# Attention scores over all 128 rows of TensorE, softmax sums applied behind the value products, and keys projected feature by feature, in a four-stage transformer kernel

## The chip, the cores and the metric

The kernel runs on one core of a Trainium2 chip. The metric is the device time of one execution in microseconds (us). Before the change three runs took 2884.61, 2885.17 and 2885.28 us; the median is 2885.17.

## What is computed

512 tokens of 1024 features pass through two layers of a block with three branches (a convolution, neighbourhood attention, window attention) that also sees 256 context tokens, then through a recurrent layer (LRU), a feed-forward layer, a layer of native sparse attention (NSA) and a second feed-forward layer. Everything is fp32. What the change touches is the attention. In short:

```python
# window attention: 8 query heads of 64, 2 key heads; blocks of 128 queries see 384 keys and the context
s_w = einsum('bqkgd,bskd->bkgqs', q_n, k_n) * scale          # masked to |distance| <= 128
s_c = einsum('bqkgd,bnkd->bkgqn', q_n, k_ctx) * scale
p = sink_softmax(concatenate([s_w, s_c], -1), sink)          # e / (sum(e) + exp(sink - m))
o = p[..., :span] @ v_n + p[..., span:] @ v_ctx

# neighbourhood attention: 8 heads, a learned bias, softmax over the neighbourhood and the context
# context tokens (first layer only): plain attention among themselves

# NSA: 16 query heads, 4 key heads; three softmaxes per query, mixed by gates
s = einsum('bgrqd,bgqkd->bgrqk', q, k) - slope[head] * distance     # causal
o = g0 * o_compressed + g1 * o_selected + g2 * o_window
```

At 512 tokens all eight blocks are selected and the window holds all tokens, so both of the last NSA softmaxes are causal attention over all earlier tokens.

## The kernel before

**Precision.** Weights, projections and scores are split: a value x becomes hi (x rounded to the type fp32r) and lo (x - hi, rounded again). A product is three matmuls, hi*hi + hi*lo + lo*hi; these are lines 141 to 143 (features on the partitions, up to 512 tokens as columns) and 152 to 154 (tokens on the partitions, 256 features as columns). `load_w` (line 117) loads a weight tile into `wr` through SP's queue, ScalarE rounds it to `wh` and VectorE subtracts to `wl`; the tags `wh` and `wl` have four buffers each. Transposes and the products of probabilities with values are plain fp32.

**Scores.** A head has 64 features. Two heads lie on the two halves of the partitions. `scores` (line 512, window attention and the context's own) and the NSA's `scores` (line 1490) issue for each of the three partial products one matmul of 64 rows per head, alternating the halves. In window attention a unit is one block of 128 queries: blocks 0 and 3 with both heads (256 context columns and 256 band columns), blocks 1 and 2 with one head at a time (256 and 384 columns). A group is one pair of heads with all its blocks, eight groups in all; the first layer has four more of two context blocks, with 256 columns each. Neighbourhood attention has its own matmuls of 512 columns at line 544, and line 517 for its context blocks.

**Softmax.** `att_sm` (line 562) takes the maximum on VectorE, adds the bias and takes the maximum again in one instruction, exponentiates on ScalarE with the sum as a by-product, inverts the sum and multiplies the probabilities by it (line 598). `att_tr` transposes them, `pv` multiplies with the values into `o`, and `finish` (line 668) multiplies `o` into the gate `U` in place.

**NSA.** `kv` projects the keys token by token (`nt_group`, 256 columns), scales them on ScalarE into both halves of `kraw`, transposes them (line 1397) and splits them into `KS`. `queries` makes the queries of a pair of heads, split into `Q`, and scales the table of distances by the two slopes into `M`. For each pair the loop at the end of `nsa` runs eight units (two branches b, query blocks 1, 3, 2, 0) and a compressed one: `scores`, `softmax`, and AHEAD units later `close` (transposes at line 1571, and for the compressed unit the products with the values at 1555 and 1559). Units have max(128*(qb+1), 256) columns: 256, 512, 384, 256. The projection of the next pair's queries is woven in as filler.

**What sets the order.** The program interleaves generators: `weave` runs a main generator and advances a filler in proportion to the cost that each step of the main one reports (ratios RA, RB and, in NSA, 0.32). The framework then schedules the instructions of all engines by dependences and its own cost estimates, so the order on an engine is not that of the source. Each engine's queue runs in order.

## Time and profile before

| | |
|---|---|
| median of three runs | 2885.17 us |
| the profiled execution, its own time | 2888.56 us |
| its span, first to last instruction | 2886.7 us |
| matmuls on PE busy | 2849.4 us, 99% |
| weight loads on PE busy | 2328.9 us, 81% |
| VectorE (DVE) busy | 1931.7 us, 67% |
| ScalarE (ACT) busy | 1119.9 us, 39% |
| GpSimd (POOL) busy | 4.4 us |
| mean granted clock of TensorE | 0.994 of full |

Matmuls are pipelined: a row's duration holds the time through the array, and the next one starts before it ends. What a matmul costs a full queue is the distance from its start to the start of the next. Attention of the block lies at about 110 to 480 us (first layer) and 1060 to 1262 us (second layer), the NSA's at 2227 to 2440 us; most of the rest is projections.

### The profile page before, as it was taken

The numbers are of one execution on the slowest core, as the hardware profiler recorded it, in microseconds if no ns is written. First come the engines' busy times: TensorE is split into PE (matmuls) and PEld (weight loads), VectorE is DVE, ScalarE is ACT, GpSimd is POOL, SyncE is SP. The second block draws the span as 40 slices with busy tenths as digits, with TensorE's granted clock in tenths as the row PEclk, the third lists the DMA queues.
The fourth block names the chain that finished last, engine by engine and source line by source line (L and its number), as shares of the span: only waits on it lengthen the run. The fifth ranks groups of instructions, "written<-read, shape, count | busy, mean of one in ns | idle before, by whom it ended". The sixth has DMA issues, their size and how long they took to land.

```text
span 2886.7 us, 41652 instructions
## 1 busy us (share of the span) xinstructions
PE 2849.4 (99%) x15936; PEld 2328.9 (81%) x15936; DVE 1931.7 (67%) x4663; ACT 1119.9 (39%) x2226; POOL 4.4 (0%) x9
## 2 busy tenths in 40 slices
PE   9999999999999999999999999999999999999998
PEld 7887877888887988778888878888888666888886
DVE  5768788994545667999747866546543777663663
ACT  4434453122222444542334742223333776322222
POOL 0000000000000000000000000000000000000000
PEclk9999999999999999999999999999999999999999
DMA  6111011321344222113233232232242001233322
GB/s 233 59 60 51 30 38 59 103 66 66 124 133 159 70 78 64 35 60 99 95 113 106 86 105 95 88 109 95 86 140 93 23 16 53 93 97 93 102 90 79
DMA packets 80119, 248.70 MB, mean 86 GB/s; under 512 B 9008, under 2 KB 16560, under 8 KB 79920
## 3 DMA queue, kind: packets, MB, share of 16 engines
q1 hardware_dynamic: 75312, 236.07, 25.2%
q10 hardware_dynamic: 4608, 9.96, 1.1%
q8 instruction: 126, 2.06, 0.3%
q14 instruction: 73, 0.60, 0.1%
HBM read 239.71 MB, written 4.19 MB: 84 GB/s over the span
## 4 chain that ended last, share of the span: by engine, by line
PE 89%; DVE 5%; issue 3%; ACT 2%; DMA 1%; POOL 0%; POOLq 0%; SPq 0%; ACTq 0%; DVEq 0%
PE g L141 21%; PE g L143 21%; PE g L142 21%; PE g L152 3%; PE g L154 3%; PE g L153 3%; PE s L517 2%; PE g L1555 1%; PE o L637 1%; PE t L613 1%; PE t L610 1%; PE s L1506 1%; PE s L544 1%; PE t L1571 1%; PE s L277 1%
## 5 line engine op out<-in xcount | busy, mean ns | idle before, releaser
L127 ACT CAST wh<-wr 128x1024 fp32r<-128x1024 f32 (+2 forms) x392 | 392.2, 1002 | 827.9 <-PE g L142 583.7
L141 PE MATMUL g<-Hh,wh 128*128 128x512 f32 x1736 | 689.7, 397 | 0.5 <-DVE Yb L1302 0.4
L142 PE MATMUL g<-Hl,wh 128*128 128x512 f32 x1736 | 681.0, 392 | 0.0
L143 PE MATMUL g<-Hh,wl 128*128 128x512 f32 x1736 | 680.3, 392 | 0.0
L128 DVE TENSOR_TENSOR wl<-wr,wh 128x1024 fp32r<-128x1024 f32 (+2 forms) x392 | 454.7, 1160 | 290.0 <-ACT wh L127 289.3
L141 PEld LDWEIGHTS g<-Hh,wh 128*128 128x128 f32 x1736 | 326.2, 188 | 73.7 <-issue 6.0
L143 PEld LDWEIGHTS g<-Hh,wl 128*128 128x128 f32 x1736 | 325.8, 188 | 71.8 <-issue 2.3
L142 PEld LDWEIGHTS g<-Hl,wh 128*128 128x128 f32 x1736 | 326.5, 188 | 64.1 <-issue 1.0
L152 PE MATMUL g<-wh,Hh 128*128 128x256 f32 x640 | 187.0, 292 | 1.3 <-ACT vn L774 1.3
L943 DVE SCALAR_TENSOR_TENSOR cv<-apad,cv 128x499 f32<-128x499 f32 (+25 forms) x305 | 187.2, 664 | 0.5
L154 PE MATMUL g<-wh,Hl 128*128 128x256 f32 x640 | 182.5, 286 | 0.0
L153 PE MATMUL g<-wl,Hh 128*128 128x256 f32 x640 | 182.3, 285 | 0.0
L141 PE MATMUL g<-fh,wh 128*128 128x512 f32 x384 | 149.4, 389 | 0.0
L142 PE MATMUL g<-fl,wh 128*128 128x512 f32 x384 | 149.4, 389 | 0.0
L143 PE MATMUL g<-fh,wl 128*128 128x512 f32 x384 | 149.4, 389 | 0.0
L152 PEld LDWEIGHTS g<-wh,Hh 128*128 128x128 f32 x640 | 122.6, 192 | 9.3 <-issue 5.5
L154 PEld LDWEIGHTS g<-wh,Hl 128*128 128x128 f32 x640 | 122.0, 191 | 4.2 <-issue 2.5
L153 PEld LDWEIGHTS g<-wl,Hh 128*128 128x128 f32 x640 | 122.6, 192 | 1.3 <-issue 0.8
L1323 DVE TENSOR_TENSOR fxp<-g,nb 128x512 f32<-128x512 f32 x48 | 33.2, 692 | 127.5 <-PE g L143 127.5
L581 ACT ACTIVATE pr<-s,m 128x512 f32<-128x512 f32 (+1 forms) x128 | 80.8, 634 | 77.0 <-DVE m L579 66.4
L1215 DVE TENSOR_TENSOR Xs<-Xs,g 128x512 f32<-128x512 f32 x48 | 33.0, 688 | 113.3 <-PE g L143 113.2
L141 PE MATMUL g<-Ch,wh 128*128 128x256 f32 x352 | 101.0, 287 | 0.0
(414 smaller groups left out, 5275.2 us busy)
## 6 DMA issues: line engine op xcount, KB each, us to landing
wr<-in_ffn_w_in_dram SPq DMA_DIRECT2D x96, 512.0 KB, 3.6
wr<-in_w_in_t_dram SPq DMA_DIRECT2D x88, 512.0 KB, 3.6
wr<-in_ffn_w_out_dram SPq DMA_DIRECT2D x64, 384.0 KB, 3.1
wada<-in_w_ada_dram SPq DMA_DIRECT2D x45, 512.0 KB, 6.0
wr<-in_w_in_n_dram SPq DMA_DIRECT2D x32, 512.0 KB, 3.7
wr<-in_lru_w_in_dram SPq DMA_DIRECT2D x20, 512.0 KB, 3.6
wr<-in_w_o_dram SPq DMA_DIRECT2D x16, 512.0 KB, 3.8
bt<-in_nab_dram SPq DMA_DIRECT2D x48, 128.0 KB, 2.5
```

The lines of the kernel that those rows point to most:

```text
L127: nc.scalar.copy(h[:, :n], r[:, :n])
L128: nc.vector.tensor_sub(lo[:, :n], r[:, :n], h[:, :n].bitcast(F32))
L141: mm(o, a, hi(k), start=k == 0, stop=False)
L142: mm(o, a, lo(k), start=False, stop=False)
L143: mm(o, b, hi(k), start=False, stop=k == KT - 1)
L152: mm(o, h, w[k][0], start=k == 0, stop=False)
L153: mm(o, h, w[k][1], start=False, stop=False)
L154: mm(o, lo(k)[:, t0:t0 + P], w[k][0], start=False, stop=k == KT - 1)
L517: nc.tensor.matmul(dst[i], Q[sl, a, qi, q0:q0 + P], K_[sl, b, ki, k0:k0 + kn], start=a + b == 0, stop=a == 1)
L581: AC.activation(pr, un["S"][i][:, :nb + 256], AF.Exp, bias=m[:, 2:3], accum_out=m[:, 3:4])
L943: V.scalar_tensor_tensor(d, src, wc, d, op0=ALU.mult, op1=ALU.add)
L1323: V.tensor_mul(xp[:, 2:514], o, rb)
```

## The change

- **Window attention and NSA scores use all 128 rows.** The queries are stored per head, with hi on one half of the partitions and lo on the other, and the keys are on both halves. One matmul then sums (hi + lo) * key; one with the keys' hi and one with their lo make the score, two matmuls per head instead of three. For this the halves that belong on the other partitions are moved by DMA: `swap` on GpSimd's queue for window attention, two transfers on SP's queue per pair of heads for NSA. Where a window unit has 256 band columns, one matmul of 512 columns takes band and context. Neighbourhood attention keeps its 64-row scores.
- **Probabilities are not normalised** in the block's attention. The sums of a group are kept side by side (`su`); `parts` inverts them once per group and spreads them over the features by matmuls with the identity, 64 columns of the array each, 8 per group (4 for a context group). `finish` multiplies them into the gate, and then the product with the values. The sink's exponential is also taken once per group. In window attention maximum and bias become one instruction over both parts, with zeros as the bias of the context.
- **NSA queries carry 0.125/slope**; the table of distances is used as it is, and the score is scaled by the slope behind the sum. The two scaled copies `M` and `Mc` are gone.
- **NSA keys are projected feature by feature** (128 features, 512 tokens as columns), so they need no transpose; a DMA on GpSimd's queue copies each to the other partitions. Weights are rearranged to match.
- **NSA's normalisation** moves from VectorE to GpSimd; half of the copies of transposed probabilities move from ScalarE to VectorE. Every fourth probability tile comes from tag `wl`. Units with 256 columns share one PSUM tile for both heads.
- AHEAD goes from 2 to 3, the NSA filler's ratio from 0.32 to 0.45, the early convolution taps' rate ET from 0.4 to 0.6. The `ones` tile shrinks to two columns.

```diff
@@ window queries: head i of a pair, hi on its own half, lo to the other
+            def to_T2_nat(raw, dst, g, tmp):
...
+                    for i, hi, lo in ((0, dst[:, 2 * pr, 0:S], tmp[:, pr]), (1, tmp[:, pr], dst[:, 2 * pr + 1, 0:S])):
+                        sl = slice(64 * i, 64 * i + 64)
+                        for (h, b), (l_, _) in zip(nat(hi[sl], tv[sl], g), nat(lo[sl], tv[sl], g)):
+                            AC.copy(h, b)
+                            V.tensor_sub(l_, b, h.bitcast(F32))
+                if g == 1:
+                    swap(dst.rearrange("p (a i) n -> p a i n", i=2), tmp, slice(0, S))
+            def swap(d4, x, c):
+                nc.gpsimd.dma_start(out=d4[64:128, :, 0, c].bitcast(F32), in_=x[0:64].bitcast(F32))
+                nc.gpsimd.dma_start(out=d4[0:64, :, 1, c].bitcast(F32), in_=x[64:128].bitcast(F32))
@@ scores
+                if not na:
+                    for i in heads:
+                        for b in range(2):
+                            kk = K_[:, b, ki, k0[0]:k0[0] + kn]
...
+                            nc.tensor.matmul(dst[i], Q[:, 2 * qi + i, q0:q0 + P], kk, start=b == 0, stop=b == 1)
+                    return
@@ att_sm
+                        for x, bias, to in todo:
+                            V.tensor_tensor_reduce(out=x, in0=x, in1=bias, scale=-1.0, scalar=mx,
+                                                   op0=ALU.add, op1=ALU.min, accum_out=to)
...
-                    rc = k.small("rc", 1)
-                    V.reciprocal(rc, tot)
...
-                        V.tensor_scalar(pr, pr, rc, None, op0=ALU.mult)
@@ new
+            def parts(grp, sinks):
...
+                V.reciprocal(y, su)
+                t = k.t_()[:, :nq * P]
+                for q in range(nq):
+                    for i in range(2):
+                        nc.tensor.matmul(t[64 * i:64 * i + 64, q * P:(q + 1) * P],
+                                         y[:, 2 * q + i:2 * q + i + 1].to_broadcast([P, 64]), k.ident,
+                                         start=True, stop=True)
+                return t
@@ attend, close
-                                finish(o, U[:, 2 * u + gr["pr"]], gr["cq"], natural)
+                                t = parts(gr, co[:, C_SINK + h0:C_SINK + h0 + 2] if natural else None)
+                                finish(t, U[:, 2 * u + gr["pr"]], gr["cq"], natural, 0.5)
+                                finish(o, U[:, 2 * u + gr["pr"]], gr["cq"], natural, 1.0)
@@ nsa, kv
-                    w = win(2 * b)
...
-                                nc.tensor.transpose(t[:, gg * P:(gg + 1) * P], raw[:, gg].rearrange("p u d -> p (u d)"), k.ident)
...
+                        o = yield from gemm_(k.load_w(a["nsa_w_k"][2 * b + f], 8, P), P, hh, hl)
+                        kr = pool.tile([P, S], F32, tag="kraw", name=k.nm("kraw"))
+                        V.tensor_mul(kr, o, rb)
+                        for i in range(2):
+                            sl, to = slice(64 * i, 64 * i + 64), slice(64 - 64 * i, 128 - 64 * i)
+                            d = KS[b][:, :, 2 * f + i]
+                            k.split(d[sl, 0], d[sl, 1], kr[sl])
+                            nc.gpsimd.dma_start(out=d[to].bitcast(F32), in_=d[sl].bitcast(F32))
@@ nsa, queries
-                V.scalar_tensor_tensor(qf, o, 0.125, rb, op0=ALU.mult, op1=ALU.mult)
...
-                    AC.activation(M[:, i], al, AF.Copy, scale=slopes[2 * f + i])
...
+                V.scalar_tensor_tensor(qf, o, co[:, D_SL + f:D_SL + f + 1], rb, op0=ALU.mult, op1=ALU.mult)
...
+                k.split(Q[0:64, 0], qx[0:64], qf[0:64])
+                k.split(qx[64:128], Q[64:128, 1], qf[64:128])
+                nc.sync.dma_start(out=Q[64:128, 0].bitcast(F32), in_=qx[0:64].bitcast(F32))
+                nc.sync.dma_start(out=Q[0:64, 1].bitcast(F32), in_=qx[64:128].bitcast(F32))
@@ nsa, scores
-                for x, y in ((0, 0), (0, 1), (1, 0)):
-                    for i in range(2):
-                        nc.tensor.matmul(S_[i][:, :nn], Q[sls[i], x, qb * P:(qb + 1) * P], KS[b][sls[i], y, g, :nn],
-                                         start=x + y == 0, stop=x == 1)
+                for i in range(2):
+                    for y in range(2):
+                        nc.tensor.matmul(S_[i][:, :nn], Q[:, i, qb * P:(qb + 1) * P], KS[b][:, y, g, :nn],
+                                         start=y == 0, stop=y == 1)
@@ nsa, softmax
-                    V.tensor_scalar(pr[:, :nk], pr[:, :nk], m[:, 2:3], GT[:, qb, h:h + 1], op0=ALU.mult, op1=ALU.mult)
+                    G.tensor_scalar(pr[:, :nk], pr[:, :nk], m[:, 2:3], GT[:, qb, h:h + 1], op0=ALU.mult, op1=ALU.mult)
```

How the instructions stand on PE, before and after, at three places. Names are tile<-moving operand,stationary operand; the numbers at a tile's name count the tiles.

First, window attention of the first layer, before: the filler of the next queries (152 to 154) and the scores of block 1 for the first head.

```order
L153 MATMUL g_3911<-wl_3808,Hh_134 128x256
L154 MATMUL g_3911<-wh_3807,Hl_135 128x256
L517 MATMUL s_3959<-kw_3080,qw_3505 128x256 x3
L517 MATMUL s_3960<-kw_3080,qw_3505 128x384 x3
L152 MATMUL g_3911<-wh_3807,Hh_134 128x256
```

The same place after (line 560 is now the scores' matmul); the second head of block 0 stands ahead of it, with band and context in one.

```order
L154 MATMUL g_3880<-wh_3771,Hl_135 128x256
L560 MATMUL s_3886<-kw_3030,qw_3455 128x512 [waits DMASW1_49]
L560 MATMUL s_3886<-kw_3030,qw_3455 128x512
L560 MATMUL s_3905<-kw_3030,qw_3455 128x256 x2
L560 MATMUL s_3906<-kw_3030,qw_3455 128x384 x2
```

Three matmuls per head and set became two, and the first to read a swapped half waits for a transfer of GpSimd's queue.

Second, the start of NSA's attention, before: the end of the first queries' projection and the first scores.

```order
L142 MATMUL g_20940<-Hl_19611,wh_20936 128x512
L143 MATMUL g_20940<-Hh_19610,wl_20937 128x512
L1506 MATMUL s_20975<-KS_20083,nQ_20967 128x256 [waits Activation_49]
L1506 MATMUL s_20976<-KS_20083,nQ_20967 128x256 [waits PE_49]
L1506 MATMUL s_20975<-KS_20083,nQ_20967 128x256
L1506 MATMUL s_20976<-KS_20083,nQ_20967 128x256
```

After, the same place (line 1604 is now the scores' matmul):

```order
L143 MATMUL g_20104<-Hh_18918,wl_20101 128x512
L141 MATMUL g_20161<-Hh_18918,wh_20157 128x512 [waits Activation_49]
L142 MATMUL g_20161<-Hl_18919,wh_20157 128x512
L143 MATMUL g_20161<-Hh_18918,wl_20158 128x512 [waits DVE_49]
L141 MATMUL g_20161<-Hh_18918,wh_20157 128x512
L142 MATMUL g_20161<-Hl_18919,wh_20157 128x512
L143 MATMUL g_20161<-Hh_18918,wl_20158 128x512
L141 MATMUL g_20161<-Hh_18918,wh_20157 128x512
L1604 MATMUL s_20139<-KS_19391,nQ_20131 128x256 [waits DMAHW6_49,DMASW4_49,PE_49]
L1604 MATMUL s_20139<-KS_19391,nQ_20131 128x256
```

Seven matmuls of the second pair's projection now stand ahead of the first score, which waits for the swap on SP's queue (DMAHW) and the copy of the keys (DMASW).

Third, the end of the second window group, second layer, before: the products with the values, then scores of the next group.

```order
L658 MATMUL o_13232<-PT_13098,misc_11922 64x256 x2
L517 MATMUL s_13270<-kw_11944,qw_12528 128x256 [waits Activation_49]
L517 MATMUL s_13271<-kw_11944,qw_12528 128x256
```

After, the end of the same group: the products, `parts` (line 681), then transposes of the next queries.

```order
L749 MATMUL o_12657<-PT_12562,misc_11493 64x256 x2
L681 MATMUL t_12676<-ident,rc_12670 64x128 [waits PE_49]
L681 MATMUL t_12676<-ident,rc_12670 64x128 x7
L527 MATMUL t_12706<-ident,raw_12542 128x128 [waits PE_49]
L527 MATMUL t_12706<-ident,raw_12542 128x128 x3
```

The eight matmuls of line 681 are new; the next group's scores come later, behind more of the filler.

## Rows read from the trace of the kernel before

**Rows 1.** The page, part 1: busy us, share of the span, instructions.
```profile
PE 2849.4 (99%) x15936; PEld 2328.9 (81%) x15936; DVE 1931.7 (67%) x4663; ACT 1119.9 (39%) x2226; POOL 4.4 (0%) x9
```

**Rows 2.** Waits of PE: who waited for whom, us, times, longest.
```profile
PE t L505 <- DVE raw L841: 3.0, 6, 0.9
PE s L1506 <- ACT nQ L209: 2.8, 2, 1.4
```

**Rows 3.** Line 1506: durations (min/median/max ns), first and last start, forms.
```profile
L1506 PE MATMUL s<-KS,nQ x384: 272/382/793, 2226.8 to 2421.9; 64*128 64x256 f32 x96, 64*128 64x512 f32 x48, 64*128 64x384 f32 x48
```

**Rows 4.** Timeline of PE, NSA attention: start us, us, instruction, count.
```profile
2287.52 0.79 PE L1506 MATMUL s<-KS,nQ 64*128 64x384 f32 x6
2288.25 0.66 PE L1571 MATMUL t<-ident,pr 128*128 128x128 f32 x4
2288.66 0.48 PE L141 MATMUL g<-Hh,wh 128*128 128x512 f32 x1
2288.97 0.40 PE L142 MATMUL g<-Hl,wh 128*128 128x512 f32 x1
...
2289.53 0.62 PE L1506 MATMUL s<-KS,nQ 64*128 64x256 f32 x6
2290.08 1.19 PE L1571 MATMUL t<-ident,pr 128*128 128x128 f32 x8
...
2293.26 0.96 PE L1506 MATMUL s<-KS,nQ 64*128 64x512 f32 x6
2294.15 0.33 PE L1571 MATMUL t<-ident,pr 128*128 128x128 f32 x1
```

**Rows 5.** Timeline of PE, projection of NSA keys and values, 256 columns.
```profile
2206.12 0.28 PE L152 MATMUL g<-wh,Hh 128*128 128x256 f32 x1
2206.24 0.28 PE L153 MATMUL g<-wl,Hh 128*128 128x256 f32 x1
```

**Rows 6.** Timeline of PE, window attention: blocks 1 and 2; then a pair.
```profile
354.25 0.61 PE L517 MATMUL s<-kw,qw 64*128 64x256 f32 x3
354.79 0.50 PE L142 MATMUL g<-Hl,wh 128*128 128x512 f32 x1
...
357.54 0.78 PE L517 MATMUL s<-kw,qw 64*128 64x384 f32 x3
358.25 0.44 PE L613 MATMUL t<-ident,pr 128*128 128x128 f32 x2
...
411.30 0.39 PE L142 MATMUL g<-Hl,wh 128*128 128x512 f32 x1
411.52 0.40 PE L143 MATMUL g<-Hh,wl 128*128 128x512 f32 x1
411.85 0.98 PE L517 MATMUL s<-kw,qw 64*128 64x256 f32 x12
412.76 0.50 PE L141 MATMUL g<-Hh,wh 128*128 128x512 f32 x1
```

**Rows 7.** Timeline of PE, NSA: compressed values, then the filler.
```profile
2284.24 1.09 PE L1559 MATMUL g<-nb,VC 124*64 124x128 f32 x13
2285.26 0.50 PE L141 MATMUL g<-Hh,wh 128*128 128x512 f32 x1
```

**Rows 8.** Timeline of all engines at the first NSA scores.
```profile
2225.36 0.69 DVE L1481 SCALAR_TENSOR_TENSOR qf<-g,nb 128x512 f32<-128x512 f32 x1 [7.45 <-PE g L143]
2226.09 0.62 ACT L209 CAST nQ<-qf 128x512 fp32r<-128x512 f32 x1 [5.35 <-DVE qf L1481]
...
2226.76 1.35 PE L1506 MATMUL s<-KS,nQ 64*128 64x256 f32 x8 [1.43 <-ACT nQ L209]
```

**Rows 9.** The page's DMA issues: tiles, count, KB each, us to landing.
```profile
bt<-in_nab_dram SPq DMA_DIRECT2D x48, 128.0 KB, 2.5
...
cD<-ct SPq DMA_DIRECT2D x4, 256.0 KB, 3.9
```

**Rows 10.** Groups of POOL: line, operation, tiles, forms, count, busy us, mean ns.
```profile
L1616 POOL TENSOR_TENSOR ht<-Xs,nb 128x512 f32<-128x512 f32 x3 | 3.7, 1271 | 2876.7 <-ACT nb L195 2876.7
```

211 lines of the change are left out of this document (134 added, 77 removed).

## The prediction

> **What bounds the kernel now.** I read the page's first part, then the waits of PE, then the timeline of PE in the stages that the diff touches. The page puts matmuls on PE in 99% of the span, DVE in 67%, ACT in 39% [rows 1]. That could be an engine that looks busy while its matmuls stretch, so the waits are the test: on the lines of attention the largest are 3.0 us in six waits and 2.8 us in two [rows 2], out of 2886.7 us. PE is the bound, its queue runs in order, and the change is priced by the distance from one PE start to the next. Work of DVE, ACT or POOL counts only where PE would wait for it.
>
> The timeline gives these distances. In a projection with 512 columns the next matmul starts 0.22 us later (411.30 to 411.52, [rows 6]); I use 0.225. With 256 columns it is 0.12 [rows 5]. For 384 columns no full-array row exists; between these two I estimate 0.172. Scores are matmuls on 64 rows (64*128 in the rows), two heads on the two halves. Six of 256 columns fill 0.55 us before the next instruction starts, six of 384 0.73, six of 512 0.89 [rows 4]. Three of 256 columns, of one head alone, fill 0.54, three of 384 0.71, and twelve of 256 0.91 [rows 6]. So two heads do share the array: six cost what three cost. But every visit to the half array has a price. From the last full matmul to the first score it is 0.33 instead of 0.22 (411.52 to 411.85, [rows 6]), 0.11 more, and the end is late too: three slots of 0.12 are 0.36, yet 0.54 to 0.55 pass.
>
> Here a rule of the Trainium skill speaks against the change. "TensorEngine Tiling (Array Packing)", Theoretical Speedup, gives a contraction of 64 or less up to twice the throughput when the array is split by rows, so going back to the full array, 4 slots for 3, would cost time. The rows agree that pairs overlap, and disagree on the balance for visits this short. The first rival below is what remains if the price of a visit doesn't go away.
>
> **Change part by part.** The times are made against the profiled execution (span 2886.7, own time 2888.56) and the difference is then taken off the median of 2885.17, which lies 3.4 below that execution.
>
> *Window attention scores (wa_att).* Before: 32 head-units alone (blocks 1 and 2 of eight groups, two heads), each with three matmuls of 256 and three of 384; 16 pairs (blocks 0 and 3) with twelve of 256; 8 context pairs with six of 256. A unit alone costs 0.11 + 0.54 + 0.11 + 0.71 = 1.47, after it 2 x 0.12 + 2 x 0.172 = 0.58: 0.89 less. In 8 of the 32 the two sets stand back to back and pay one visit, so there I count 0.68. That is 24 x 0.89 + 8 x 0.68 = 26.8. A pair costs 0.11 + 0.91 = 1.02, after it four of 512, 0.90: 16 x 0.12 = 1.9. A context pair costs 0.11 + 0.55, after it 0.48: 8 x 0.18 = 1.4. **Together -30.** If all units stood back to back it would be -25.
>
> *NSA scores.* 64 units: 32 of 256 columns save 0.66 - 0.48 = 0.18, 16 of 384 save 0.84 - 0.69 = 0.15, 16 of 512 save 1.00 - 0.90 = 0.10. **-9.8.** If the visit cost only its entry, 0.11, and the late end stayed whatever stands there, this part would lose about 2.
>
> *NSA keys.* Before: 192 matmuls of 256 columns, 23.0, and eight sets of four transposes. A set costs 0.41, and the projection matmul behind it takes 0.31 instead of 0.225 (2288.25 to 2288.97, [rows 4]): 0.50. After: 96 matmuls of 512 columns, 21.6, no transposes. **-1.4 - 4.0 = -5.4.** The copies of the keys to the other partitions go out on POOL's queue. The value projection of the same branch, 96 matmuls of 0.12 or 11.5 us, follows on PE before any score asks for them, so I take them at nothing; without that cover each branch would cost a landing, 2.5 to 3.9 [rows 9].
>
> *Sums behind the value products (parts).* It adds 8 matmuls of 128 columns to each of 16 groups and 4 to each of 8 context groups: 160, into half the columns (128*64). No row is this form; the nearest are the 124*64 ones of NSA, 13 in 1.02 = 0.078 [rows 7]. **+12.5.** Ends: half a transpose, 0.05 (two at a time), 8; a whole one, 0.10, 16 (four in 0.41, [rows 4]).
>
> *DVE and ACT.* Gone are a normalisation per head-unit and its small operations; added are one product with PSUM per group and three small operations. PE waits 3.0 us at most for any one DVE line here [rows 2], so I take this at nothing; it can only help.
>
> *NSA queries.* Slopes go into the queries, which removes two scaled copies of the table per pair of heads from ACT: nothing, PE covers it. But each pair's second halves now go through two DMAs on SP's queue. For the first pair nothing covers them. Before: the first score starts 1.40 after the product qf [rows 8]. After: qf 0.69, cast 0.62 [rows 8], a subtraction like qf's, 0.69, then a landing between 2.5 and 3.9 [rows 9], so 4.5 to 5.9. The order shows seven projection matmuls (1.6) put ahead of that score. Net 1.5 to 2.9 later; with the second head's half a cast later I take **+2.4**. For the later pairs the next projection ends several us earlier than the scores, so one of the two waits of 1.4 [rows 2] goes: **-1.4**. Behind a swap on SP stand weight loads that are two tiles ahead: nothing.
>
> *Window queries* are swapped by POOL's queue, four times on the way. The order puts 56 matmuls of 256 columns (6.7) between the last transpose and the first score in the first layer, 11 of 256 and 24 of 512 (6.7) in the second. The chain beneath is about four subtractions, each no longer than the cast of 0.62 [rows 8], and a landing of up to 3.9 [rows 9]: 6.4. Just covered: nothing.
>
> *Normalisation of NSA on POOL.* 128 instructions, 5120 columns for each of eight pairs of heads. POOL's only row is a product of two tensors, 1.27 for 512 columns [rows 10]: 12.7 per pair at most, 102 of the 195 us of that stage (2226.8 to 2421.9, [rows 3]). AHEAD goes from 2 to 3, so a unit has another unit's time. Nothing.
>
> **Sum:** -30 - 9.8 - 5.4 + 12.5 + 2.4 - 1.4 = -31.7. The profiled execution would be 2856.9, the median 2853.5; **I forecast 2854**, with 2844 to 2866 for this case from the ends above.
>
> **Rivals.** *The visit's price stays (slower).* If the late starts come from changing between the two number formats that the projections and the transposes have, and not from the halves, the scores are slots alone: NSA gains one slot per unit, 32 x 0.12 + 16 x 0.172 + 16 x 0.225 = +10.2; pairs of window attention 16 x (0.90 - 0.72) = +2.9, context pairs 8 x 0.12 = +1.0, units alone -32 x 0.292 = -9.3; with -5.4, +12.5 and the queries' +1.0 that is +13: 2898. It decides below about 0.09 us per visit. Against it: the 0.11 stands between a projection and scores, which share a format [rows 6]. It is also what the Trainium skill's rule on splitting the array by rows would leave here. 0.07.
>
> *The swaps aren't covered (no change).* Four window swaps and eight NSA swaps; if each is late by 2.6 us, the gain is gone: 2885. For it: POOL's queue has no DMA row in this profile, and the window's cover is thin. Against it: the scheduler put covering work there. 0.09.
>
> *POOL sets the pace of NSA.* If 512 columns took 2.5 us, twice its row, a pair of heads would take 25 on POOL against 23 on PE (195 / 8, less 1.2): 8 x 2 = +16, 2870. Against it: that is far from its only row. 0.07.
>
> *More than the sum.* `parts` two at a time (-4), the DVE waits gone (-3), window swaps helping nothing: 2846. 0.14.
>
> **How the numbers follow.** The forecast has 0.63. A measurement of this kernel tells 0.2%, 5.8 us, from no change. Faster by more: 0.63 + 0.14 + 0.06 of the POOL case's 0.07 = 0.83; within: the uncovered swaps and a rest, 0.09; slower: 0.08. The range leaves out the slower rival, the uncovered swaps and the far ends: 2836 to 2878.
>
> **What would show it.** Right: score rows as 128*128, four per NSA unit, starting 0.12 to 0.225 apart, no 0.11 before them; 160 new matmuls under 0.1 apart; no transposes of keys; POOL under 0.8 us per 512 columns or below 1.3 anyway. Wrong: PE waiting for DMA landings at the first score of each pair of heads, or for POOL before the transposes of `pr`; or scores at 0.3 us and more apart.

## The result and the profile after

The changed kernel takes 2924.99 us (median of four runs, 2921.07 to 2926.49); the kernel before, run beside it on the same chip, 2885.23. The ratio is 1.0132, 95% interval [1.0119, 1.0145]: **39.8 us slower**, where 31 us faster was forecast.

| | before | after |
|---|---|---|
| profiled execution, its own time | 2888.56 us | 2926.49 us |
| its span | 2886.7 us | 2924.7 us |
| mean granted clock of TensorE | 0.994 | 0.991 |

Part 1 of the page of after, which answers to [rows 1]:

```profile
PE 2865.0 (98%) x15792; PEld 2345.7 (80%) x15792; DVE 1875.2 (64%) x4175; ACT 1084.7 (37%) x2088; POOL 105.8 (4%) x159
```

VectorE (DVE) has 56 us less to do and ScalarE (ACT) 35, as intended; matmuls on PE are 144 fewer, and yet PE is busy 16 us longer. So PE does less and takes longer for it. A stretch whose code the change does not touch shows it. The timeline of PE in the first feed-forward layer, before:

```profile
1999.99 0.39 PE L143 MATMUL g<-Hh,wl 128*128 128x512 f32 x1
2000.21 0.39 PE L141 MATMUL g<-Hh,wh 128*128 128x512 f32 x1
2000.44 0.39 PE L142 MATMUL g<-Hl,wh 128*128 128x512 f32 x1
2000.67 0.39 PE L143 MATMUL g<-Hh,wl 128*128 128x512 f32 x1
2000.89 0.39 PE L141 MATMUL g<-Hh,wh 128*128 128x512 f32 x1
```

The same of after:

```profile
1999.84 0.39 PE L143 MATMUL g<-Hh,wl 128*128 128x512 f32 x1
2000.07 0.40 PE L141 MATMUL g<-Hh,wh 128*128 128x512 f32 x1
2000.31 0.39 PE L142 MATMUL g<-Hl,wh 128*128 128x512 f32 x1
2000.54 0.40 PE L143 MATMUL g<-Hh,wl 128*128 128x512 f32 x1
2000.78 0.39 PE L141 MATMUL g<-Hh,wh 128*128 128x512 f32 x1
```

Four steps from start to start take 0.90 us before and 0.94 after. No instruction of these lines was changed, no wait stands in the rows, and the granted clock is 1.00 in both. Over the whole trace, the matmuls of 512 columns of lines 141 to 143 that follow one another within 0.3 us start 227.7 ns apart on average before (7449 of them, five in six at 226 or 227) and 232.7 after (7592, nearly all from 228 to 241). This distance is called the pitch below. 7592 x 5.0 ns = 38 us, nearly the whole loss. The steps of 256 columns (lines 152 to 154) are 119.6 ns before and 118.7 after.

What the change did to these lines is only to move their operands. The tile of ones shrank from 128 columns to 2 (512 bytes per partition to 8, which take up 32) and the table of columns grew by 8 columns (32 bytes). Both stand ahead of the weights and the activations and moved them alike, by 448 bytes. The new sums (`su`, 384 bytes) stand between the weights and the activations and moved the activations alone. So the distance between the two grew by 384 bytes, which is 128 modulo 256. In bytes from the start of a partition, by the two built programs:

```
                       before            after             modulo 256: before   after
stationary  wh, wl     27136 and on      26688 and on                       0      64
moving      Hh, Hl     62208, 78592      62144, 78528                       0     192
moving      fh, fl     137984, 162560    137920, 162496                     0     192
```

The other signs of the prediction came true in part. NSA's scores in the timeline of PE of after:

```profile
2313.78 0.39 PE L143 MATMUL g<-Hh,wl 128*128 128x512 f32 x1
2314.01 0.64 PE L1604 MATMUL s<-KS,nQ 128*128 128x256 f32 x4
2314.49 0.27 PE L1676 MATMUL t<-ident,pr 128*128 128x128 f32 x1
```

Four full-array matmuls in 0.48 us, entered 0.23 after the projection, against 0.55 and an entry of 0.33 before [rows 4, 6]. The price of a visit is gone, as forecast. But PE waits in new places. The waits of PE of after, whole span (who waited for whom, us, times, longest):

```profile
PE g L141 <- ACT wh L127: 6.4, 7, 2.5
...
PE s L1604 <- ACT pr L1642: 3.7, 6, 0.6
...
PE s L560 <- DMA qw<-bt: 3.4, 2, 2.9
```

Before, the largest in NSA was 2.8 us in two [rows 2]; now a projection waits for its weights' cast, a score for ACT to have read the PSUM tile that it is to fill, and a window score for a swapped query.

### The profile page after: what moved, and what is told of

It is laid out like the page before. It is cut to its first block, busy times and chain, and to the rows that moved or that the text cites. A ratio compares the mean times of both kernels' runs of the same rounds, so it can differ in the third digit from the quotient of the medians.

```text
span 2924.7 us, 41020 instructions
## 1 busy us (share of the span) xinstructions
PE 2865.0 (98%) x15792; PEld 2345.7 (80%) x15792; DVE 1875.2 (64%) x4175; ACT 1084.7 (37%) x2088; POOL 105.8 (4%) x159
## 4 chain that ended last, share of the span: by engine, by line
PE 86%; issue 5%; DVE 5%; ACT 2%; DMA 1%; POOL 0%; POOLq 0%; ACTq 0%; SPq 0%; DVEq 0%
PE g L141 21%; PE g L143 21%; PE g L142 21%; PE g L152 3%; PE g L154 2%; PE g L153 2%; PE g L1660 1%; PE s L560 1%; PE o L728 1%; PE t L1676 1%; PE t L704 1%; PE s L1604 1%; PE t L701 1%; PE s L592 1%; DVE wl L128 1%
## 5 line engine op out<-in xcount | busy, mean ns | idle before, releaser
L141 PE MATMUL g<-Hh,wh 128*128 128x512 f32 x1768 | 709.2, 401 | 6.5 <-ACT wh L127 6.4
L142 PE MATMUL g<-Hl,wh 128*128 128x512 f32 x1768 | 701.2, 397 | 0.0
L143 PE MATMUL g<-Hh,wl 128*128 128x512 f32 x1768 | 699.9, 396 | 0.4 <-DVE wl L128 0.4
L1043 DVE SCALAR_TENSOR_TENSOR cv<-apad,cv 128x503 f32<-128x503 f32 (+22 forms) x277 | 172.9, 673 | 0.4
L152 PE MATMUL g<-wh,Hh 128*128 128x256 f32 x576 | 168.4, 292 | 1.9 <-ACT vn L869 1.3
L153 PE MATMUL g<-wl,Hh 128*128 128x256 f32 x576 | 163.2, 283 | 1.8 <-DVE wl L128 1.8
L154 PE MATMUL g<-wh,Hl 128*128 128x256 f32 x576 | 163.1, 284 | 0.0
L152 PEld LDWEIGHTS g<-wh,Hh 128*128 128x128 f32 x576 | 109.1, 189 | 9.7 <-issue 5.1
L153 PEld LDWEIGHTS g<-wl,Hh 128*128 128x128 f32 x576 | 109.1, 189 | 2.6 <-DVE wl L128 2.1
L660 ACT ACTIVATE pr<-s,su 128x512 f32<-128x512 f32 (+1 forms) x128 | 80.8, 635 | 81.8 <-DVE su L657 52.2
```

The costliest lines, as they stand in the source:

```text
L141: mm(o, a, hi(k), start=k == 0, stop=False)
L142: mm(o, a, lo(k), start=False, stop=False)
L143: mm(o, b, hi(k), start=False, stop=k == KT - 1)
L152: mm(o, h, w[k][0], start=k == 0, stop=False)
L153: mm(o, h, w[k][1], start=False, stop=False)
L154: mm(o, lo(k)[:, t0:t0 + P], w[k][0], start=False, stop=k == KT - 1)
```

## The experiments

Theory A: the places of the tiles cost some 38 us, and what is left of the change is worth little, because the PE work that it saves comes back as waits. Theory B: the loss comes from what the change adds (GpSimd's DMA queue, the products of the sums, a lower clock). Each ratio is to the kernel before, run beside it. Kernels that build on e1 have its tiles on multiples of 256 bytes.

### Where the tiles stand (e1 to e4, e11, e17)

**e1**: the changed kernel with its tiles back on multiples of 256. The small tiles, the sums among them, now stand ahead of the weights, so they are no longer between weights and activations.

```diff
         self.const = pool(name="const", bufs=1)
+        self.sm = pool(name="sm", bufs=4)
+        self.pad = pool(name="pad", bufs=1)
         self.wp = pool(name="wp", bufs=1)
         self.pp = pool(name="pp", bufs=1, space=PSUM)
-        self.sm = pool(name="sm", bufs=4)
...
+        nc.vector.memset(self.pad.tile([P, 16], F32, name="pad"), 0.0)
```

> The changed kernel; only the order of the pools of small tiles and weights is swapped and 64 bytes per partition are left free, so that the weights and all the activations behind them start at multiples of 256 bytes again, as they did before the change (weights 29440 and on, Hh 62208, fh 137984). No instruction is added or moved, but for one memset at the start. Theory A (the smaller tile of ones moved every tile behind it by 64 bytes, and TensorE's matmuls of 512 columns in lines 141 to 143 come every 232.7 ns in place of 227.7): 7592 recorded matmuls x 5.0 ns = 38 us come back, 2925 - 38 = 2887, anywhere from 2875 to 2895, and their pitch is 226 to 227 ns again. Theory B (the loss comes from what the change adds: DMAs on GpSimd's queue, the sums' products, a lower clock): 2920 to 2930 and a pitch of 232 to 233 ns.

Measured: 2889.09 us, ratio 1.0013 [1.0004, 1.0023]; pitch 227.7 ns. 35.9 of the 39.8 us are back. What was expected names the tile of ones as what had moved the tiles; the next run shows that it is not.

**e2**: the kernel before, with the tile of ones alone made smaller.

```diff
-        self.ones = self.const.tile([P, P], F32, name="ones")
+        self.ones = self.const.tile([P, 16], F32, name="ones")
...
```

> The kernel before; the tile of ones alone is cut from 128 columns to 16 (512 to 64 bytes per partition; the product that used all of it reads one column 128 times, and the idle products at waits take the identity). Every tile behind it stands 448 bytes lower, so the weights are where the changed kernel has them (18496 and on) and Hh is at 61760, 64 over a multiple of 256. Nothing else differs. Theory A (where the tiles stand): 7449 matmuls x about 5 ns = 37 us slower, 2885 + 37 = 2922, from 2910 to 2930, with a pitch of 232 to 233 ns. Theory B (what the change adds): 2885 within 3 us.

Measured: 2886.19, ratio 1.0001 [0.9991, 1.0010], pitch 227.7. A miss for theory A as it was put: Hh stood 64 over a multiple of 256 and cost nothing, because the weights stood 64 over as well. The smaller tile of ones alone costs nothing.

**e3** adds to e2 `self.pad.tile([P, 112], ...)` between the small tiles and the activations (only the weights are off).

> As the run before with the small tile of ones, but 448 bytes are left free ahead of the activations, so that these stand where the kernel before has them (Hh 62208, fh 137984) and only the weights are off (18496 and on, 64 over a multiple of 512). Theory A1 (the stationary operand's place matters): about 2922 with a pitch of 232 to 233 ns, as when all are shifted. Theory A2 (the moving operand's place matters): 2885 and 227 ns. A3 (how the two stand to each other): off by 64 to each other, so slow here too, at a pitch that may differ from that of all shifted. Theory B: 2885.

Measured: 2918.91, ratio 1.0115 [1.0098, 1.0132], pitch 233.3.

**e4** is the kernel before with `self.pad.tile([P, 16], ...)` at that place (only the activations are off).

> The kernel before with 64 bytes left free ahead of the activations: the weights stand where they did (multiples of 512), Hh at 62272 and fh at 138048, 64 over a multiple of 256. Theory A1 (the stationary operand): 2885, pitch 227 ns. A2 (the moving operand): about 2922, pitch 232 to 233 ns. A3 (how the two stand to each other): slow here and with the weights shifted alone, and less so with both shifted. Theory B: 2885.

Measured: 2889.73, ratio 1.0012 [1.0003, 1.0021], pitch 229.2.

Taken together, sorted by the start of the moving operand less that of the stationary one, modulo 256 bytes:

| kernel | distance | mean pitch, 512 columns | mean step, 256 columns, lines 152 to 154 of before | time |
|---|---|---|---|---|
| before; e1; e2 | 0 | 227.7 ns in each | 119.6; 119.7; 119.6 ns | 2885; 2889; 2886 us |
| e4 | 64 | 229.2 | 115.4 | 2890 |
| after | 128 | 232.7 | 118.7 | 2925 |
| e3 | 192 | 233.3 | 117.3 | 2919 |

A3 holds for 512 columns: neither operand's own place decides, but the distance of the two. The steps of 256 columns go the other way: off distance 0 they get shorter, in lines 152 to 154, where the weights are the moving operand, and in lines 141 to 143 too (119.5 ns before, 116.9 in e4, 116.0 in e3). In e4 the two cancel: against e2, the steps of 512 columns sum to 11.5 us more and those of 256 to 12.5 less, so PE's work is the same, and what it is slower by is idle time (31.3 us in place of 27.7). In e3 it is 41.7 more and 10.4 less. So the pitch of 512 columns alone doesn't give the time.

A row of the source view shows it without any working out (durations of a matmul, min/median/max, first and last start). Of before, after, e1, e3 and e4 in turn:

```profile
L142 PE MATMUL g<-fl,wh x384: 389/389/389, 1861.7 to 2870.5; 128*128 128x512 f32 x192
```

```profile
L142 PE MATMUL g<-fl,wh x384: 390/393/404, 1872.9 to 2908.6; 128*128 128x512 f32 x192
```

```profile
L144 PE MATMUL g<-fl,wh x384: 389/389/389, 1858.1 to 2870.2; 128*128 128x512 f32 x192
```

```profile
L144 PE MATMUL g<-fl,wh x384: 393/394/398, 1873.2 to 2899.8; 128*128 128x512 f32 x192
```

```profile
L144 PE MATMUL g<-fl,wh x384: 392/393/394, 1859.7 to 2871.2; 128*128 128x512 f32 x192
```

389 flat at distance 0, 392 to 394 at 64, 393 to 398 at 192, 390 to 404 at 128. The first start lies early in the first feed-forward layer, the last at the end of the second: between them after loses 27 us on before (1035.7 against 1008.8; NSA lies in between).

One run holds both cases. `lul`, an operand of the LRU's last projection, stood 192 over before; the 64 bytes of e4 put it at distance 0 while they took `fl` off it. Of before and e4:

```profile
L142 PE MATMUL g<-lul,wh x80: 393/394/506, 1671.6 to 1728.8; 128*128 128x512 f32 x80
```

```profile
L144 PE MATMUL g<-lul,wh x80: 387/389/500, 1669.8 to 1725.5; 128*128 128x512 f32 x80
```

And of 256 columns with the weights moving, of before and e4:

```profile
L152 PE MATMUL g<-wh,Ch x192: 277/283/387, 86.7 to 1122.4; 128*128 128x256 f32 x192
```

```profile
L154 PE MATMUL g<-wh,Ch x192: 276/276/388, 86.8 to 1117.5; 128*128 128x256 f32 x192
```

**e11** applies this to operands that were off in the kernel before too (`V.memset(one("gap", 16), 0.0)` ahead of the LRU's tile, 8 more columns for NSA's KC).

> As e1, but the three more moving operands that weren't on multiples of 256 bytes before the change either are put there too: the two halves of the LRU's input to its last projection (luh, lul, at 192 over) and NSA's keys and result (KS, nus, at 224 over), with 64 and 32 bytes left free ahead of them. If what counts is the distance between the moving and the stationary operand, modulo 256 bytes: their pitch falls from 231 to 236 ns to 227, 240 x 7 + 255 x 7 = 3.4 us, and the 64 scores of 512 columns from 233 to 227: 2885, from 2883 to 2887. If those pitches have another cause: 2889.

Measured: 2885.42, ratio 0.9998 [0.9989, 1.0007]. The row of line 144 of e1 and of e11:

```profile
L144 PE MATMUL g<-lul,wh x80: 393/394/503, 1667.8 to 1725.2; 128*128 128x512 f32 x80
```

```profile
L144 PE MATMUL g<-lul,wh x80: 389/389/498, 1667.8 to 1723.7; 128*128 128x512 f32 x80
```

From start to start these went from 230 to 236 ns to 226 or 227. The rows are plain; of the time, the two intervals overlap.

**e17** does the same to the kernel before.

> The kernel before with only the places of luh, lul, KS and nus moved to multiples of 256 bytes: the same 3.5 us as between e1 and e11, 2886.3 - 3.5 = 2882.8, from 2881 to 2884. Against e14 this leaves what the window part of the change is worth by itself: 2 to 3 us by the sum of e6 and e11, 17 by the prediction's terms.

Measured: 2884.93, ratio 0.9993 [0.9984, 1.0001]: 1.5 us by the medians, less than expected and within what the runs can tell.

What happens inside PE is not shown by any run; shown is that the pitch follows the distance. The Trainium skill ("SBUF — State Buffer", Who interferes with whom) gives PE two read ports, one for the moving operand and one for loading weights, and calls them independent. Read so, the distance between the two operands should not matter. The measurement differs and decides: 227.7 or 233.3 ns by that distance. That the ports are the place where it happens is not shown.

### Is the rest worth what was forecast? (e5 to e8, e16, e18)

e1 is the change without the accident of places, and it is 3 us slower than before, not 31 faster. Its trace (an execution of 2887.64 us, 1.5 below its median) against that of before (2888.56, some 3 above its own, so that the two stand level here), by distances from start to start, split into the time up to a matmul's end and the idle time behind it:

| stretch | work | idle |
|---|---|---|
| first layer, to the first merge | -7.0 | 9.7 to 13.3: +3.6 |
| second layer, to the merge | -6.4 | 4.2 to 10.5: +6.2 |
| NSA, from the keys to the last score | -12.7 | 5.7 to 19.3: +13.6 |
| sum | **-26.1** | **+23.4** |

The prediction's terms for work, -30 - 9.8 - 5.4 + 12.5, are -32.7. So PE's work fell by most of what was forecast, and nine tenths of that came back as idle time.

**e5** makes no products of the sums; each unit scales its exponentials on DVE.

```diff
...
+                    V.reciprocal(n[:, 3:4], su)
+                    V.tensor_scalar(pr, pr, n[:, 3:4], None, op0=ALU.mult)
...
-                                t = parts(gr, co[:, C_SINK + h0:C_SINK + h0 + 2] if natural else None)
-                                finish(t, U[:, 2 * u + gr["pr"]], gr["cq"], natural, 0.5)
-                                finish(o, U[:, 2 * u + gr["pr"]], gr["cq"], natural, 1.0)
+                                finish(o, U[:, 2 * u + gr["pr"]], gr["cq"], natural, 0.5)
```

> The changed kernel with the tiles on multiples of 256 bytes as in e1 (2889), and without the products that spread the sums of exponentials: each head-unit's exponentials are scaled on DVE ahead of the transposes again, as before the change, with the sink's exponential and the sums per unit. The full-array scores stay. In the profile of e1 the 320 products of `parts` take 24.7 us from start to next start (192 x 0.0765 + 128 x 0.078). Theory P (PE is the bound in attention, so these 24.7 us are paid in full): 2889 - 25 = 2864, from 2858 to 2872. The prediction's count (160 products, 12.5 us) would give 2876. Rival D (DVE was relieved for a reason: with the scaling back, PE waits for DVE ahead of the transposes): 2880 or more, with new waits of PE on the line of the scaling.

Measured: 2904.84, ratio 1.0064 [1.0049, 1.0079], 16 us above e1. The time is rival D's. The window scores of the second layer and the merge behind them, busy us of PE, weight loads, DVE, ACT and POOL, then the granted clock; before, e1 and e5:

```profile
1160.00:1290.00 130.00, 129.88 (x710) 92.86 (x711) 118.62 (x417) 67.91 (x193) 0.00 (x0) 1.00 0.14 46
```

```profile
1160.00:1290.00 130.00, 125.11 (x702) 99.02 (x703) 112.59 (x288) 66.08 (x174) 2.35 (x4) 0.99 0.18 54
```

```profile
1160.00:1290.00 130.00, 118.75 (x598) 87.48 (x596) 113.43 (x353) 68.60 (x197) 2.35 (x4) 0.96 0.15 45
```

DVE is at 67% of the whole span [rows 1], but at 118.6 of 130 us here before, 91%, and at 113.4 in e5. It has the masks, the copies of the transposes, the splits of the swapped queries and the taps of the convolution. With the scaling added, PE is idle 11 us of the 130 and its granted clock is 0.96. Over the whole execution PE's idle time is 17 us above e1's (68.2 against 50.9), and the mean granted clock 0.987 in place of 0.993, which I estimate at up to 17 us (0.006 x 2905). That takes back the 25 us of the products and more. D's sign did not come: no large wait of PE stands on the line of the scaling. The largest new ones are for ACT (3.2 us for the merge's `th`, 2.6 for exponentials in the first layer) and for DVE's splits at the merge (2.7). So that DVE's queue is what makes them is argued, not shown.

**e6** undoes the NSA part as a whole (lines 1486 on and `AHEAD` as before the change).

> As e1, with the whole NSA part as before the change (scores on 64 rows, keys by transposes, slopes in the tables, scaling on DVE, all copies on ACT, two units ahead); the window part stays changed. Theory W (the NSA part saves 12.7 us of PE's work and loses 13.6 in new waits, read from e1 against before in the stretch from the compressed keys to the last score): 2889 - 1 = 2888, from 2884 to 2892, and the gaps of that stretch go from 19 us to 6. The prediction's terms (-9.8 - 5.4 + 2.4 - 1.4 = -14): without it 2889 + 14 = 2903.

Measured: 2883.06, ratio 0.9986 [0.9977, 0.9996], 6.0 us below e1 and 1 below W's range: NSA's part costs time, a little more than theory W said. The idle time of that stretch fell from 19.3 to 6.3 us, as W had it.

**e7** leaves NSA's new matmuls and gives back the engines: `G.tensor_scalar` to `V.tensor_scalar` at the scaling, `(V.tensor_copy if i else AC.copy)` to `AC.copy`.

> As e1, but in NSA the scaling of the exponentials goes back from GpSimd to DVE and all the copies of the transposed tiles back to ACT; the rest of the NSA part stays changed. Theory W1 (GpSimd's slower scaling, 0.69 us in place of 0.44, makes the exponentials late, and with them the transposes and the next scores): most of the 8 to 10 us of waits inside the pairs of heads go, 2880 to 2883. Theory W2 (ACT's order makes them: the casts of the next weights and the exponentials stand behind the two casts of the queries, which wait for the projection): the two waits of 0.6 per pair stay, and with 27 us of copies more on ACT the time is 2888 to 2895.

Measured: 2894.26, ratio 1.0028 [1.0017, 1.0039]. The time is W2's, its sign is not: the two waits of 0.6 per pair nearly went. In the stretch of the pairs (2226 to 2427 us) PE waits 1.6 us in four for the weights' cast, where e1 has 3.9 in six, and 0.6 in two for exponentials, where e1 has 3.8 in six. In their place it waits 7.2 us for ACT's copies of the transposes. The idle time of NSA's stretch stayed (19.3 and 19.5 us); the granted clock of 2140 to 2440 us fell from 0.99 to 0.97.

**e8** is e5 and e6 together.

> e5 and e6 together: tiles on multiples of 256 bytes, full-array scores in window attention with the scaling on DVE and no products of the sums, NSA as before the change. If the two parts add up (theories P and W): 2889 - 25 - 1 = 2863, from 2857 to 2872. If DVE becomes late (rival D): 2879 or more. By the prediction's terms for scores alone (-30): 2855.

Measured: 2894.52, ratio 1.0025 [1.0015, 1.0036]: 11 us above e6, so D's time again.

**e16** scales on DVE in the neighbourhood attention only; NSA is as before the change and all operands stand as in e11 (this base is e14, below: 2880.11).

> As e14 (2880.1), but in the neighbourhood attention the exponentials are scaled on DVE again and the products of the sums are made for window attention alone: 160 of the 320 products go from PE, 160 x 0.077 = 12.3 us, and about 160 scalings (0.5 us each) come back to DVE, which is busy 132 of 212 us in that stage of the first layer in e1 and was at 151 before the change. If PE is the bound there: 2880 - 12 = 2868, from 2866 to 2873. If DVE's turn makes PE wait as in e5 (which gained 5 us in that stage of the first layer and lost 13 in the second layer's attention): 2876 to 2885.

Measured: 2873.75, ratio 0.9953 [0.9940, 0.9965]: 6.4 us below e14, half of what the products take.

**e18** also puts `ET` back to 0.4.

> e16 with the pace of the convolution's taps woven into window attention at 0.4 in place of 0.6, as before the change, so that DVE has fewer of them while the window scores are made and more behind them. If DVE's share there (some 90%) makes the waits of PE: 2 to 5 us below e16. If the taps left over make the next merge late: 2 to 5 us above.

Measured: 2871.43, ratio 0.9947 [0.9933, 0.9960]. It is 2.3 us below e16, but the intervals overlap, so ET's part is not shown. This beats both kernels: 15 us below before and 54 below after. Part 1 of its page:

```profile
PE 2820.8 (98%) x15888; PEld 2329.4 (81%) x15888; DVE 1907.7 (67%) x4357; ACT 1116.1 (39%) x2184; POOL 12.3 (0%) x23
```

It has the window part's scores over all rows, the products of the sums in window attention alone, NSA as before, and the operands at distance 0 as in e11.

### Which waits (e9, e10, e12 to e15)

In e1 six of the eight pairs of heads in NSA lose two waits of some 0.6 us. The same in after, ACT's timeline:

```profile
2293.60 0.62 ACT L209 CAST nQ<-qf 64x512 fp32r<-64x512 f32 x1
2294.12 0.68 ACT L1642 ACTIVATE pr<-s,m 128x512 f32<-128x512 f32 x1
...
2295.58 0.61 ACT L209 CAST qx<-qf 64x512 fp32r<-64x512 f32 x1
...
2296.51 1.05 ACT L127 CAST wh<-wr 128x1024 fp32r<-128x1024 f32 x1
```

and PE's:

```profile
2294.05 0.27 PE L1676 MATMUL t<-ident,pr 128*128 128x128 f32 x1
2294.94 0.62 PE L1604 MATMUL s<-KS,nQ 128*128 128x256 f32 x3 [0.62 <-ACT pr L1642]
...
2297.61 0.50 PE L141 MATMUL g<-Hh,wh 128*128 128x512 f32 x1 [0.57 <-ACT wh L127]
```

The cast of the queries (`nQ`, 2293.60) stands ahead of the exponentials (2294.12), and the score at 2294.94 needs the PSUM tile that they read. The second cast (`qx`, 2295.58) stands ahead of the next weights' cast (2296.51), and the projection at 2297.61 needs those.

**e9** puts both casts on DVE.

```diff
-                k.split(Q[0:64, 0], qx[0:64], qf[0:64])
-                k.split(qx[64:128], Q[64:128, 1], qf[64:128])
+                for hi, lo, src in ((Q[0:64, 0], qx[0:64], qf[0:64]), (qx[64:128], Q[64:128, 1], qf[64:128])):
+                    V.tensor_copy(hi, src)
+                    V.tensor_sub(lo, src, hi.bitcast(F32))
```

> As e1 (2889), but the two casts of each pair of heads' queries in NSA run on DVE in place of ACT; nothing else differs. Theory W2 (ACT's order makes the new waits of NSA: the cast of the next weights and the exponentials of the units ahead stand behind the casts of the queries, 2 x 0.62 us): the two waits that come once per pair, 0.57 before the projection and 0.63 before a score, go, and the 2.5 before the second pair's projection shrinks by a cast: 7 x 1.2 + 0.6 to 2.5 = 9 to 11 us, 2878 to 2881. If they come from the scaling on GpSimd or from having three units open: 2887 to 2891, with both waits still there.

Measured: 2899.65, ratio 1.0045 [1.0030, 1.0060]. The waits of PE in that stage, e1 and then e9:

```profile
PE g L143 <- ACT wh L129: 3.9, 6, 1.1
PE s L1606 <- ACT pr L1644: 3.8, 6, 0.6
```

```profile
PE t L1679 <- DVE PT L1682: 7.7, 6, 1.6
PE g L145 <- DVE wl L130: 3.2, 1, 3.2
PE s L1607 <- ACT pr L1645: 3.1, 6, 0.5
...
PE g L143 <- ACT wh L129: 0.6, 1, 0.6
```

The wait for the weights' cast went, as W2 said; 7.7 us for DVE's copies and 3.2 for its low halves of the weights came. Moving the casts moved the wait; the one for the exponentials stayed.

**e10** makes the low halves of the weights on GpSimd during the block's attention.

```diff
-                nc.vector.tensor_sub(lo[:, :n], r[:, :n], h[:, :n].bitcast(F32))
+                getattr(self, "lo_eng", nc.vector).tensor_sub(lo[:, :n], r[:, :n], h[:, :n].bitcast(F32))
...
+        k.lo_eng = nc.gpsimd
...
+        k.lo_eng = nc.vector
```

> As e1, but while the two attention stages run, the low halves of the weights (weight less its rounded half, 1.2 us of DVE for 1024 columns) are made on GpSimd instead of DVE. Theory D (in window attention DVE is nearly full too: 142.5 of the 160 us from 1160 to 1320 in e1, 148.6 before the change, so PE's saving there can't be had): about 12 such products per 130 us go, in both layers some 50 us of DVE in all, and the stages shorten by part of it, 2879 to 2885. Theory E (DVE isn't what binds): 2887 to 2891. If GpSimd at 2.5 us per 1024 columns is too slow or slows DVE by its own reads: 2893 or more, with waits of PE for the low halves.

Measured: 2925.07, ratio 1.0138 [1.0121, 1.0154], the third outcome. GpSimd's group of line 130 from 110 to 320 us, and in the same stretch small products of DVE (8 columns; min/median/max):

```profile
L130 POOL TENSOR_TENSOR wl<-wr,wh 128x1024 fp32r<-128x1024 f32 x14 | 33.5, 2394 | 167.4 <-ACT wh L129 167.4
```

```profile
L167 DVE TENSOR_TENSOR rs_a<-rs_y x20: 150/166/2247, 128.5 to 317.5; 128x8 f32<-128x8 f32 x14, 128x4 f32<-128x4 f32 x6
```

2394 ns for what DVE does in 1224, and a DVE product of 166 ns took 2247: it began 0.2 us behind the start of one of GpSimd's and ended with it. So this run could not lighten DVE, and says nothing on theory D. The Trainium skill ("SBUF — State Buffer", Who interferes with whom) has DVE's second input share a port with GpSimd, as a lock for a whole instruction; the trace agrees, by that 2247.

**e12** sets `AHEAD` to 2.

> As e1 (2889), but NSA keeps two units of scores open in place of three, as before the change. Theory Q (the third open unit takes the last of the four PSUM tiles of scores, so that once per pair of heads a score waits 0.63 us for ACT to have read one): those seven waits go, 4 us, 2884 to 2886. Theory R (the third unit is what gives GpSimd's slower scaling its time): the transposes wait for the scaled exponentials instead, 0.25 us a unit or more, 2891 to 2905.

Measured: 2888.60, ratio 1.0008 [0.9998, 1.0017]: no difference in time from e1. In the waits both came. Of 2226 to 2427 us, where e1 has the 3.9 and 3.8 shown under e9:

```profile
PE t L1678 <- POOL pr L1646: 4.7, 9, 0.7
PE t L1678 <- DVE PT L1681: 4.6, 5, 0.9
PE t L1678 <- ACT PT L1681: 2.9, 7, 0.7
PE s L1606 <- ACT pr L1644: 0.2, 1, 0.2
```

The two waits per pair are gone, so they need the third open unit, as Q said. The transposes wait for GpSimd's scaling and for copies instead, as R said (0.9 us in two for GpSimd in e1), and that eats the gain.

**e13** and **e14**: NSA as before the change, with all operands as in e11; e13 keeps the new keys.

> The window part changed, of the NSA part only the keys made feature by feature; scores, queries, scaling and order of NSA as before the change; all moving operands on multiples of 256 bytes as in e11. Against the same kernel with the keys as before (e14): the prediction's term for the keys is -5.4. Of it the waits at the two new key weights (0.4 + 0.9 and 0.7 + 0.9 us in the profile of e1) would leave -2.5. By the one or the other 2874 to 2877, if e14 is at 2879.5.

> e6 (window part changed, NSA as before the change; 2883.1) with all moving operands on multiples of 256 bytes as in e11 (which came out 3.7 below e1). The two don't touch the same instructions, but for NSA's scores: 2883.1 - 3.7 = 2879.4, from 2877 to 2882.

Measured: e13 2882.18, 0.9984 [0.9975, 0.9993]; e14 2880.11, 0.9982 [0.9972, 0.9991]. e14 is where the sum of e6 and e11 put it. The keys alone are worth nothing that these runs can tell, where 2.5 to 5.4 us were expected. In NSA's stretch PE's work is 2.8 us less in e13 than in e14 and its idle time 2.9 us more; PE waits 3.2 us there for the weights of the value projections that follow the new keys (1.8 for their low halves, 1.4 for their casts).

**e15** sends the window queries' copies from SP's queue.

> As e1, but the copies of the window queries' halves to the other partitions go out on SP's queue in place of GpSimd's. In e1 they land after a median of 3.6 us on GpSimd's queue (8 of them), and the first window score of the second layer waits 3.2 us for one; the like copies of NSA's queries land after 2.2 us on SP's. Theory S (the landing is on the path): 1.4 us less at that place and a little less of the lower clock behind it, 2887 to 2888. Theory T (the wait is set by DVE, which makes the halves late, and SP's queue holds weight loads ahead of the copies): 2889 or more.

Measured: 2888.31, ratio 1.0010 [1.0001, 1.0020]: no difference from e1 that can be told, so theory S's 1.4 us are not shown. In e1's timeline of all engines the copy is issued late:

```profile
1168.17 0.59 POOL L520 DMA_DIRECT2D qw<-bt  x1 [25.11 <-DVE rs_y L171]
...
1171.85 0.47 PE L562 MATMUL s<-kw,qw 128*128 128x512 f32 x1 [3.19 <-DMA qw<-bt]
```

PE waits 3.19 us, until 1171.85, for a copy issued at 1168.17.

## Why the prediction was wrong

**The step that failed first: "I use 0.225".** The distance between matmuls of 512 columns was taken from rows of before as a property of the form, and all unchanged projections were carried over at no cost. It is a property of the two operands' places too, and the change moved these: 35.9 of the 71 us between forecast and result (after against e1). The edit that did it, the 384 bytes of the new sums between the weights and the activations, has no term in the prediction at all, though the change names the sums. The smaller tile of ones did not do it (e2). No row at distance 0 could have told the price; but some rows of before could: luh, lul and nus, which stand off, had steps of 231 to 236 ns there, and the prediction has no row of them.

The other 35 us lie between the forecast and e1. By the profiled executions it is 30.8 (2887.64 against 2856.9): 22.4 of idle time, 6.6 of work and some 2 outside the three stretches.

**`parts`, +12.5.** Mis-sized by two. The 160 products appear as 320 matmuls, 24.7 us in e1. Of after:

```profile
L681 PE MATMUL t<-ident,rc x320: 272/273/323, 144.6 to 1275.6; 128*64 128x128 f32 x160
```

[rows 7] gave the price of one row of the trace, 0.078, and the program's instructions were counted. Line 1559 itself has 64 instructions in the program and 128 matmuls in the trace: an fp32 product is two there, a transpose one. e16 got 6.4 of the 12.3 us of the neighbourhood attention's half by moving it to DVE.

**Window scores, -30, and NSA scores, -9.8.** The rows bear out the price of 256 columns: 0.48 for four, no late entry. In NSA four of 384 took 0.79 to the next start and four of 512 0.94, where 0.69 and 0.90 were used. Window attention's work fell by 13.4 with the products in it, where -17.5 was forecast: without them it fell by 38, more than -30, and that made good most of the error in `parts`. Which matmuls gave the 8 more is not shown, so this is luck. NSA's work fell by 12.7, where -15.2 was forecast. The first rival did not come.

**NSA keys, -5.4.** Not borne out: e13 is no faster than e14. The prediction asked only whether the copies of the keys are covered; what came is PE waiting for the weights of the value projections that were to cover them, 3.2 us in e13 and 2.9 in e1.

**"Nothing" for ACT, DVE, GpSimd and the swaps.** This is the second failure: +23.4 us of idle time where +1.0 (2.4 - 1.4) was forecast. The sentence was that their work counts only where PE would wait for it, and that PE waits 3.0 us at most for any line. That told how things stood with PE's old work. Taking 26 us of work from PE shortened the cover of every chain beside it. In window attention DVE was busy 91% of a stretch in which PE was idle for 0.1 us; that it then sets the pace fits the times of e5 and e8, but their waits don't show it. In NSA the queries' longer chain (two casts, two subtractions, two transfers) stands in front of exponentials and weights. The prediction costed its DMA landing and its first pair, but not who is queued behind its casts on ACT for the others (7.7 us in e1).

**The swaps just covered.** In the second layer they were not: 4.0 us in three waits, the longest 3.19, most of that stretch's 6.2. From issue to the score it was 3.7, close to the landing of 3.9 that the prediction used as its end. The rival's size (2.6 each, twelve of them) did not come.

**Normalisation of NSA on GpSimd: nothing.** Held, and for the reason given, that a unit more is open: PE waits 0.9 us for it in e1, and 4.7 with two units open (e12). e7, which takes it back, also moves copies to ACT and tells nothing on it alone.

**The first pair, +2.4, and the second pair's stall, -1.4.** The stall went as forecast: the second pair's first score (2250.12 us in e1) follows without a wait, where it was 1.41 us late before. No first score waits for a landing either. PE stands earlier, at the second pair's projection. Of e1, ACT and then PE:

```profile
2221.47 0.62 ACT L211 CAST nQ<-qf 64x512 fp32r<-64x512 f32 x1 [5.47 <-DVE qf L1578]
2222.00 1.04 ACT L129 CAST wh<-wr 128x1024 fp32r<-128x1024 f32 x1
```

```profile
2223.09 0.50 PE L143 MATMUL g<-Hh,wh 128*128 128x512 f32 x1 [2.50 <-ACT wh L129]
...
2226.31 1.48 PE L1606 MATMUL s<-KS,nQ 128*128 128x256 f32 x4
```

The cast of that projection's weights (`wh`) stands behind the queries' (`nQ`). That 2.5 us is near +2.4 is luck; the mechanism was another.

What stays open: how much of NSA's idle time each link makes. The two waits per pair need the third open unit (e12), and the one for the weights also the casts on ACT (e9), but each time other waits took their place, and no run took the whole away but e6. Why the granted clock falls more in some runs (e5, e7) is also open.

## What to carry to other kernels

Before pricing what an edit does, print where every tile starts with and without it: a small tile that is added moves all that is allocated behind it against all that stands ahead, and here that was worth more than the rest of the change. Take prices from rows, but count in the same rows: ask how many records of the trace one instruction of the program makes. And when work is taken from the engine that bounds, read the next engine's share in that stretch, not over the span, since the stretch can't get shorter than that engine's work; and ask of each chain beside it which engine's queue it stands in and what is queued behind.

## What the runs showed of the hardware that was not expected

- The step of an fp32r matmul of 512 columns is 227.7 ns when the moving and the stationary operand start a multiple of 256 bytes apart, 229.2 at 64 over, 232.7 at 128 and 233.3 at 192. Shifting both alike costs nothing (e2). With 256 columns (lines 152 to 154) it goes the other way: 119.6 ns at distance 0, 115.4 in e4, 117.3 in e3.
- A plain fp32 product is two matmuls in the trace (line 1559: 64 instructions, 128 rows), a plain transpose one.
- In e10 a DVE product of 8 columns took up to 2247 ns in the first layer while GpSimd made a product of 1024 columns, 166 otherwise.
- After the wait of 3.19 us in the second layer the granted clock is 0.91 over 1160 to 1180 us in e1, where it is 1.00 before.
